# Order of the projected tiles around the HGRN2 heads and the RWKV-7 preparation in a two-layer decoder trunk

## The chip, the cores and the metric

The kernel runs on one core of one Trainium2 chip. The metric is the device time of one execution in microseconds; three executions are shown and their median counts. One execution was taken with the hardware profiler.

## What is computed

Two layers work on a sequence of 512 tokens of width 1024 in float32. Per layer:

```
h    = x * (1 + scale) + shift              (adaLN of the conditioning vector c)
proj = h @ w_in                             (49 column tiles of 128)
q, f, i, z_hg   -> HGRN2, 4 heads of 128    S_t = diag(f_t) S_{t-1} + k_t v_t^T, o_t = S_t^T q_t
                   v = i, k and log f from f, in chunks
r, k, v, z_rw, w, a -> RWKV-7, 8 heads of 64   (token shift on all of them)
y    = (sigmoid(g_A) * y_A + sigmoid(g_B) * y_B) @ w_out
x    = LayerNorm(alpha * x + gate * y)
```

HGRN2's head needs f for its gate f and its key k, q for the query, and i only as the value v. The RWKV-7 preparation needs r, k and v of its two heads.

## The kernel before, in words

Everything is kept transposed, features in partitions and 512 tokens in the free dimension. One projected tile is 128 columns of `w_in` against all of h: `proj` (L252) loads the weights in two halves, splits each into a rounded part (ACT, L120) and a remainder (POOL, L125), and issues 24 matmuls of 512 columns (L261, L262, L266) into one PSUM bank of the pool `pj`, which has two banks. A tile's reader must have emptied a bank before the tile after next may begin.

Each layer runs, for p = 0 to 3, first `hg_head` (L688), one HGRN2 head, and then `rw_prep` (L403), which prepares two RWKV heads. Both are chains of small steps on DVE, ACT and POOL with few matmuls, written as Python generators. `weave` (L277) mixes them with a second generator, the fill, which is the projection of tiles needed later: before part i of the chain it takes `counts[i]` matmuls from the fill, and `issue_after` ties the part's own PE instructions behind the last of them. What is left of the fill runs after the chain. The order on PE is thus written out by hand; the order on the other engines is laid down when the kernel is built, by priority (the order in which the program traces the instructions) among those that are ready and have a buffer. All engine queues are worked off in order.

In `hg_head` the parts are: (1) copies of I and Q, the tanh of F, the gate f and the key K (L697 to L704); (2) four transposes of I (L709) and a copy, then the reciprocal of f's odd columns (L720) and products with f; (3) the first product (L730) and its mask; (4) to (8) five levels that double the block, each with two matmuls (L759), a predicated copy into `acc` (L761), copies of K and Q (L751, L754) and products by `double`; (9) a last level (L775); (10) transposes of K (L785); (11) L792 and the states S; (12) the output products L802 and L805. PSUM pool `hg` has two banks. In `rw_prep` the first part holds the shifts of r, k and v, the second the transposes of L438, the third the products L454 and L455, the fourth L487 and the transposes of v (L494).

Before, the fill of head p is R, K and V of p (72 matmuls; in layer 0 the first R and K come from the start, and I of head 1 joins), and the fill of preparation p is I, Q and F of head p+1 (72), of which `WPR` puts 0 + 4 + 26 + 5 between the parts and 37 come after it. In layer 1 the tiles WA, I and Q are computed at the layer boundary (`next_tiles`, L914) and F runs by itself in front of head 0. The adaLN reductions (L302, with their loads at L321) are filled in on DVE where `ada_next` (L313) places them. Loads of weights are issued on SP's queue (L246).

Of the kernel before, what the change touches and what calls it, by code (L numbers as in the profile page):

```python
# [22 lines left out]
NWARM = 5  # L23
ORD = ((11, 2), (3, 20), (4,), (5, 6), (21,7), (8,), (), ())

WHZ = (0, 2, 0, 7, 0, 15, 5, 0, 7, 1, 7, 12)
WHG = (0, 4, 16, 6, 11, 6, 6, 0, 8, 0, 6, 12)
WPR = (0, 4, 26, 5)
WHN = (0, 19, 0, 11, 11)
WT = (172, 0, 13, 0, 14, 3, 0, 0)  # L30
WCH = (0, 3, 3, 1, 7, 5, 5)
# [50 lines left out]
def body(ctx, tc, d):  # L82
# [20 lines left out]
    def u(shape=(128, 512), dt=F32):  # L103
        return st("u", list(shape), dt)
# [580 lines left out]
        hilo(y, o)  # L685


    def hg_head(l, hd, pf, pq, pi, outs):  # L688


        D_ = dv[l]
        h1, h1n, lbm = (D_[n][:, hd:hd + 1] for n in ("h1", "h1n", "lbm"))
        iv, Qb, Q, th = u(), u(), hl(), u()

        c4 = lambda t, e: t.rearrange("p (c e j) -> p c e j", c=2, e=2)[:, :, e]
        k4 = lambda t, e: c4(t, 1)[:, :, ::-1] if e else c4(t, 0)
        for e in range(2):  # L697
            A.copy(k4(iv, e), c4(pi, e))
        A.copy(Qb, pq)
        act(th, pf, AF.Tanh, scale=0.5)  # L700
        K, f = hl(), u()
        ts(V, f, th, 1.0, h1, ALU.add, ALU.mult)
        ts(V, f, f, lbm, 1e-30, ALU.add, ALU.max)
        ts(G, K, th, h1n, h1, ALU.mult, ALU.add)  # L704

        yield
        pT = ps("hg")
        for t in range(4):
            PE.transpose(pT[:, t * 128:(t + 1) * 128], iv[:, t * 128:(t + 1) * 128], ident)  # L709
        vt = hl()  # L710
        A.copy(vt, pT)
        acc = hl()
        c3 = lambda t: t.rearrange("p (c j) -> p c j", j=128)
        acc3 = c3(acc)
# [31 lines left out]
        for n, H in enumerate(HG_LEVELS):  # L746

            late = lambda t: t.rearrange("p (c b two j) -> p c b two j", c=4, two=2, j=H)[:, :, :, 1]
            lv = u()
            kp, ql = lv[:, 0:256], lv[:, 256:512]  # L750
            A.copy(ql.rearrange("p (c b j) -> p c b j", c=4, j=H), late(Q))  # L751
            for e in range(2):
                k = k4(K, e).rearrange("p c (m f j) -> p c m f j", f=2, j=H)[:, :, :, e]
                PK[e](kp.rearrange("p (c m f j) -> p c m f j", c=2, f=2, j=H)[:, :, :, e], k)  # L754
            w = double(H, w)
            yield
            pS = ps("hg")
            for c in range(2):
                mm(pS[:, c * 128:(c + 1) * 128], kp[:, c * 128:(c + 1) * 128], ql[:, c * 128:(c + 1) * 128],  # L759
                   start=c == 0, stop=c == 1)  # L760
            V.copy_predicated(late(acc), hmask[:, n].rearrange("p (c b j) -> p c b j", c=4, j=H),  # L761
                              pS[:, 0:256].rearrange("p (c b j) -> p c b j", c=4, j=H))
        lv = u()
        kp, ql = lv[:, 0:256], lv[:, 256:512]
        A.copy(ql.rearrange("p (c j) -> p c j", j=64), c3(Q)[:, :, 64:128])
# [13 lines left out]
            A.copy(c4(acc, e)[r, :, 64:128], c4(pS[:, 0:256], e)[r])  # L779
        dec = W[:, w:w + 4]  # L780

        yield
        pT = ps("hg")
        for t in range(3):
            PE.transpose(pT[:, t * 128:(t + 1) * 128], (kr if t == 1 else K[:, t * 128:(t + 1) * 128]), ident)  # L785
# [43 lines left out]

    xs, x1, out = d["x"], d["x1"], d["out"]  # L830
    w_in = d["w_in"]
    first = (CT_WA, CT_I, CT_Q, CT_F, CT_K, CT_R, CT_GH)
    NF = len(first)
    rtag = ("raw", "raw", "raw", "o", "o", "o", "o", "pu", "pu", "pu", "pu", "o", "o", "o")
    utag = (("wh", "wl"), ("wh", "wl"), ("wh", "wl"), ("hl", "hl"), ("hl", "hl"), ("hl", "pr"), ("pr", "pr"),
# [77 lines left out]

    def next_tiles():  # L914

        srcs = [w_in[1, c, h] for c in (CT_WA, CT_I, CT_Q) for h in range(2)]
        tags = (("wh", "wl"), ("wh", "wl"), ("wh", "wl"), ("G", None), ("G", None), ("X", "X"))
        ws, vw = [], []

        def unit():  # L920
            n = len(ws)
            if n == 2 and not vw:
                raw, w = st("raw", [128, 8, 32]), st("bkt", [128, 8, 64], F32R)
                nc.sync.dma_start(raw, d["vdn"])
                act(w[:, :, 0:32], raw, AF.Copy)
                tt(G, w[:, :, 32:64], raw, w[:, :, 0:32].bitcast(F32), ALU.subtract)
                vw.append(w)
                return
            th, tl = tags[n]
            raw = st("raw", [128, 512])  # L930
            nc.sync.dma_start(raw, srcs[n])
            if tl:
                hi, lo = st(th, [128, 512], F32R), st(tl, [128, 512], F32R)
            else:
                g = st(th, [128, 2, 512], F32R)
                hi, lo = g[:, 0], g[:, 1]
            split(raw, hi, lo)
            ws.append((hi, lo))
        def tiles():
            fo.extend([ps("rw"), ps("rw"), ps("pj"), ps("pj")])  # L940
            for th in range(2):
                tk = slice(256 * th, 256 * th + 256)
                for n, o in enumerate(fo):
                    if n == 1:
                        for k in range(8):
                            w = vw[0][:, k]
                            if k < 7:
                                yield mm(o[0:64, tk], w, hT[k][:, 0, tk], start=th == 0 and k == 0, stop=False)
                            yield mm(o[0:32, tk], w[:, 0:32], hT[k][:, 1, tk], start=False, stop=False)
                        yield mm(o[0:64, tk], w, hT[k][:, 0, tk], start=False, stop=th == 1)  # L950
                        continue
                    for k in range(8):
                        hi, lo = (w[:, k % 4 * 128:k % 4 * 128 + 128] for w in ws[2 * (n - (n > 1)) + k // 4])
                        yield mm(o[:, tk], hi, hT[k][:, 0, tk], start=th == 0 and k == 0, stop=False)
                        yield mm(o[:, tk], hi, hT[k][:, 1, tk], start=False, stop=False)
                        yield mm(o[:, tk], lo, hT[k][:, 0, tk], start=False, stop=th == 1 and k == 7)

        fo = []
        return fo, unit, tiles()
# [3 lines left out]
    for l in range(L):  # L963
# [44 lines left out]
                outs.append((yield from ct(c)))  # L1008

        if l == 0:  # L1010
            hgp, rkv = [fout[1], fout[2], fout[3]], [fout[5], fout[4]]
        else:
            hgp, rkv = [fout[2], fout[3]], []
            run(tiles([CT_F], hgp))
        for p in range(NP):
            fill = tiles([c + p for c in (CT_R, CT_K, CT_V)][len(rkv):], rkv)
            pi, pq, pf = hgp
            early = []
            if l == 0 and p == 0:
                fill = itertools.chain(fill, tiles([CT_I + 1], early))  # L1020
            weave(hg_head(l, p, pf, pq, pi, oT), fill, WHZ if l == 0 and p == 0 else WHG)
            run(fill)
            ada_next(*itertools.islice(ada, (WAZ, WAO)[l][2 * p]))
            if p == 0:
                rw["vtm"] = [st("X", [128, 512]) for _ in range(8)]
            hgp = early
            if p < 3:
                fill = tiles([c + p + 1 for c in (CT_I, CT_Q, CT_F)][len(hgp):], hgp)
            else:
                fill = itertools.chain.from_iterable(  # L1030
                    [gate(j) for j in range(5)] + [zrw(p) for p in range(NP)] + [zhg(p) for p in range(NP)] +
                    [gate(j) for j in range(5, KT)])
            weave(rw_prep(l, p, *rkv), fill, WPR)
            ada_next(*itertools.islice(ada, (WAZ, WAO)[l][2 * p + 1]))
            if p < 3:
                run(fill)
            rkv = []
# [293 lines left out]
```

## Time and profile before

| | us |
|---|---|
| three executions | 1029.41, 1031.85, 1032.98 |
| median | 1031.85 |
| the profiled execution, its own time | 1030.67 |
| span of its profile, first to last instruction | 1028.9 |

The span is the profiled execution from its first to its last instruction; 1.8 us of that execution lie around it. A busy share is an engine's share of the span. The granted clock of PE is 1.00 at 2.4 GHz and 0.50 at 1.2 GHz, the only two levels; a value between them is a mean over a stretch. An operation on a timeline is shown with the idle time of its engine just before it and with what ended that idle time. Matmuls overlap in the pipeline: one of 512 columns lasts longer than the distance to the next one.

### The profile page before, as it was taken

To read this page: it belongs to the slowest core of one execution; us is meant where nothing else is said; L and a number is where in the kernel's file an instruction comes from. 1 tells how busy PE (TensorE), PEld (TensorE's weight loads), DVE (VectorE), ACT (ScalarE), POOL (GpSimd) and SP (SyncE) were. 2 spreads that over 40 slices of the span, in tenths; PEclk is the share of its full clock that TensorE was granted. 3 is DMA by queue.
4 is the path that set the end of the run, shared out by engine and by line. 5 is a ranking of instruction groups with operands and counts; after the bars stand their busy time and mean duration, and the time that the engine had idled before them with its cause. 6 is when DMAs were issued, how large, how long until landed. Compare 5 with 4: busy or idle time off the path is not lost.

```text
span 1028.9 us, 16689 instructions
## 1 busy us (share of the span) xinstructions
PE 951.9 (93%) x6132; PEld 761.9 (74%) x6132; DVE 700.1 (68%) x1251; ACT 454.3 (44%) x920; POOL 578.9 (56%) x502
## 2 busy tenths in 40 slices
PE   7988898989989999989999988989999999998997
PEld 4766677878877777757887777777787777776876
DVE  7789986577993444694677867676799544384347
ACT  3456354546325335423356455445642443444321
POOL 5465545345445656768545554545554466576765
PEclk9989899999999999999999999999999999998999
DMA  9824532223321111674535322322232111254422
GB/s 310 301 84 146 170 104 71 80 65 83 92 73 52 53 42 54 194 250 133 184 124 175 113 82 62 83 67 68 62 97 88 53 50 45 92 164 133 123 83 82
DMA packets 61748, 112.83 MB, mean 110 GB/s; under 512 B 6865, under 2 KB 11361, under 8 KB 61666
## 3 DMA queue, kind: packets, MB, share of 16 engines
q1 hardware_dynamic: 57778, 105.12, 33.2%
q10 hardware_dynamic: 3888, 6.64, 2.0%
q8 instruction: 48, 0.79, 0.3%
q14 instruction: 34, 0.28, 0.1%
HBM read 106.49 MB, written 5.25 MB: 109 GB/s over the span
## 4 chain that ended last, share of the span: by engine, by line
PE 44%; DVE 40%; issue 6%; POOL 5%; DMA 3%; ACT 2%; POOLq 0%; DVEq 0%; ACTq 0%; SPq 0%
PE ppj L266 9%; PE ppj L261 9%; PE ppj L262 9%; DVE t L125 4%; DVE z L302 4%; DVE hl L125 3%; DVE t L523 3%; POOL wl L125 3%; DVE u L125 2%; DVE B L302 2%; DVE ar L526 2%; DVE t L515 2%; DVE u L134 1%; PE prw L579 1%; DMA z<-in_w_ada 1%
## 5 line engine op out<-in xcount | busy, mean ns | idle before, releaser
L125 POOL TENSOR_TENSOR wl<-raw,wh 128x512 fp32r<-128x512 f32 (+1 forms) x233 | 318.6, 1372 | 255.7 <-PE ppj L266 107.0
L120 ACT ACTIVATE wh<-raw 128x512 fp32r<-128x512 f32 (+1 forms) x233 | 144.1, 622 | 159.9 <-PE ppj L262 105.1
L261 PE MATMUL ppj<-B,wh 128*128 128x512 f32 x432 | 174.4, 404 | 4.5 <-ACT wh L120 3.9
L262 PE MATMUL ppj<-B,wh 128*128 128x512 f32 x432 | 172.4, 399 | 0.0
L261 PE MATMUL ppj<-A,wh 128*128 128x512 f32 x400 | 164.1, 410 | 5.6 <-ACT t L122 3.7
L262 PE MATMUL ppj<-A,wh 128*128 128x512 f32 x400 | 162.7, 407 | 0.0
L266 PE MATMUL ppj<-B,wl 128*128 128x512 f32 x432 | 126.0, 403 | 2.1 <-POOL wl L125 2.1
L266 PE MATMUL ppj<-A,wl 128*128 128x512 f32 x400 | 117.9, 407 | 1.7 <-POOL wl L125 1.6
L261 PEld LDWEIGHTS ppj<-B,wh 128*128 128x128 f32 x432 | 82.0, 190 | 24.0 <-ACT wh L120 5.9
L262 PEld LDWEIGHTS ppj<-B,wh 128*128 128x128 f32 x432 | 82.1, 190 | 16.2
L261 PEld LDWEIGHTS ppj<-A,wh 128*128 128x128 f32 x400 | 77.4, 193 | 22.5 <-ACT t L122 4.1
L266 PEld LDWEIGHTS ppj<-B,wl 128*128 128x128 f32 x432 | 79.5, 190 | 19.2 <-POOL wl L125 3.8
L262 PEld LDWEIGHTS ppj<-A,wh 128*128 128x128 f32 x400 | 77.5, 194 | 15.4
L266 PEld LDWEIGHTS ppj<-A,wl 128*128 128x128 f32 x400 | 74.5, 192 | 17.6 <-POOL wl L125 3.0
L125 POOL TENSOR_TENSOR hl<-hl,u 128x256 f32<-128x256 f32 x40 | 33.9, 847 | 40.9 <-DVE u L754 24.6
L125 DVE TENSOR_TENSOR t<-t,t 128x144 f32<-128x144 f32 (+29 forms) x62 | 44.8, 723 | 2.1
L759 PE MATMUL phg<-u 128*128 128x128 f32 x160 | 27.7, 300 | 15.6 <-DVE hl L761 13.5
L759 PEld LDWEIGHTS phg<-u 128*128 128x128 f32 x160 | 24.1, 204 | 23.4 <-ACT u L768 14.6
L131 DVE TENSOR_SCALAR u<-u,dvh 128x512 f32<-128x512 f32 x8 | 8.0, 997 | 44.9 <-ACT u L122 44.9
L302 DVE CUSTOM_DVE_ANT_0 z<-z,mbd,prm 128x512 f32<-128x512 f32 x32 | 29.2, 912 | 5.9 <-DMA z<-in_w_ada 3.2
L125 DVE TENSOR_TENSOR hl<-hl,u 128x256 f32<-128x256 f32 x64 | 31.8, 516 | 0.5
L125 DVE TENSOR_TENSOR raw<-raw,X 128x512 f32<-128x512 f32 x8 | 5.9, 742 | 38.5 <-DMA raw<-in_w_out 31.9
(475 smaller groups left out, 1982.4 us busy)
## 6 DMA issues: line engine op xcount, KB each, us to landing
raw<-in_w_in SPq DMA_DIRECT2D x182, 256.0 KB, 2.6
z<-in_w_ada SPq DMA_DIRECT2D x64, 256.0 KB, 3.4
B<-in_w_ada SPq DMA_DIRECT2D x16, 512.0 KB, 6.2
raw<-in_w_br SPq DMA_DIRECT2D x32, 256.0 KB, 2.7
raw<-in_w_out SPq DMA_DIRECT2D x32, 256.0 KB, 3.0
u<-in_x SPq DMA_DIRECT2D x8, 256.0 KB, 3.9
o<-in_w_in SPq DMA_DIRECT2D x14, 128.0 KB, 4.5
t<-in_xt SPq DMA_DIRECT2D x6, 256.0 KB, 3.2
```

Of the source, the lines that this page charges most:

```text
L120: A.activation(out, in_, f, scale=scale)
L125: e.tensor_tensor(o, a, b, op=op)
L134: V.scalar_tensor_tensor(o, a, s, b, op0=op0, op1=op1)
L261: yield mm(o, w, xh, start=half == 0 and k == 0, stop=False)
L262: yield mm(o, w, xl, start=False, stop=False)
L266: yield mm(o, w, xh, start=False, stop=half == n - 1 and k == 3)
L302: V.tensor_tensor_reduce(out=w[h], in0=w[h], in1=silc[h], scale=0.5, scalar=0.0 if h else init, op0=ALU.mult, op1=ALU.add, accum_out=part[ ...
L515: V.transpose(Tin[qs].rearrange("p t s -> p s t"), ax[qs, :, cs_].rearrange("p h s -> p s h"))
L523: V.tensor_reduce(blk(R, t, [32, j]), pv, axis=AX.X, op=ALU.add)
L526: V.transpose(ax[qs, :, cs_].rearrange("p h t -> p t h"), R[qs].rearrange("p j t -> p t j"))
L579: mm(pg[h][:, p * 128:(p + 1) * 128], BK[p][hs, ch], ZR[p][hs, ch], start=p == 0, stop=p == 3)
L759: mm(pS[:, c * 128:(c + 1) * 128], kp[:, c * 128:(c + 1) * 128], ql[:, c * 128:(c + 1) * 128], start=c == 0, stop=c == 1)
```

## The change

The tile order turns round. The fill of preparation p is now F and Q of head p+1 (48 matmuls), and I of a head is projected first in the fill of that head itself, before K, R and V (96 matmuls). In layer 0, preparation 0, all three are still projected there (F in head 0, then Q and I). Layer 1's boundary computes F in place of I, and F no longer runs by itself. In `hg_head` the tanh of F comes first; the copies of I come at its start if I is there, or in the third level; the transposes of I join the third level's group of matmuls; the transposes of K join the last level's. The parts of `hg_head` become 10 in place of 12, and the counts of all weaves over heads and preparations are new.

```diff
--- before.py
+++ after.py
@@ -23,9 +23,11 @@
 NWARM = 5
 ORD = ((11, 2), (3, 20), (4,), (5, 6), (21,7), (8,), (), ())
 
-WHZ = (0, 2, 0, 7, 0, 15, 5, 0, 7, 1, 7, 12)
-WHG = (0, 4, 16, 6, 11, 6, 6, 0, 8, 0, 6, 12)
-WPR = (0, 4, 26, 5)
+WHZ = (0, 4, 4, 4, 6, 6, 7, 7, 5, 5)
+WHG = (0, 14, 5, 7, 8, 8, 9, 9, 7, 8)
+WHL = (0, 26, 4, 6, 7, 7, 9, 9, 7, 8)
+WHS = (0, 10, 4, 5, 6, 6, 7, 8, 6, 6)
+WPR = (0, 4, 20, 6)
 WHN = (0, 19, 0, 11, 11)
 WT = (172, 0, 13, 0, 14, 3, 0, 0)
 WCH = (0, 3, 3, 1, 7, 5, 5)
@@ -685,30 +687,31 @@
         hilo(y, o)
 
 
-    def hg_head(l, hd, pf, pq, pi, outs):
+    def hg_head(l, hd, src, outs):
 
 
         D_ = dv[l]
         h1, h1n, lbm = (D_[n][:, hd:hd + 1] for n in ("h1", "h1n", "lbm"))
-        iv, Qb, Q, th = u(), u(), hl(), u()
+        pf, pq = src[:2]
+        Qb, Q, th = u(), hl(), u()
 
         c4 = lambda t, e: t.rearrange("p (c e j) -> p c e j", c=2, e=2)[:, :, e]
         k4 = lambda t, e: c4(t, 1)[:, :, ::-1] if e else c4(t, 0)
-        for e in range(2):
-            A.copy(k4(iv, e), c4(pi, e))
+        iv = []
+
+        def values():
+            iv.append(u())
+            for e in range(2):
+                A.copy(k4(iv[0], e), c4(src[2], e))
+
+        act(th, pf, AF.Tanh, scale=0.5)
+        if len(src) > 2:
+            values()
         A.copy(Qb, pq)
-        act(th, pf, AF.Tanh, scale=0.5)
         K, f = hl(), u()
         ts(V, f, th, 1.0, h1, ALU.add, ALU.mult)
         ts(V, f, f, lbm, 1e-30, ALU.add, ALU.max)
         ts(G, K, th, h1n, h1, ALU.mult, ALU.add)
-
-        yield
-        pT = ps("hg")
-        for t in range(4):
-            PE.transpose(pT[:, t * 128:(t + 1) * 128], iv[:, t * 128:(t + 1) * 128], ident)
-        vt = hl()
-        A.copy(vt, pT)
         acc = hl()
         c3 = lambda t: t.rearrange("p (c j) -> p c j", j=128)
         acc3 = c3(acc)
@@ -753,6 +756,8 @@
                 k = k4(K, e).rearrange("p c (m f j) -> p c m f j", f=2, j=H)[:, :, :, e]
                 PK[e](kp.rearrange("p (c m f j) -> p c m f j", c=2, f=2, j=H)[:, :, :, e], k)
             w = double(H, w)
+            if n == 2 and not iv:
+                values()
             yield
             pS = ps("hg")
             for c in range(2):
@@ -760,6 +765,13 @@
                    start=c == 0, stop=c == 1)
             V.copy_predicated(late(acc), hmask[:, n].rearrange("p (c b j) -> p c b j", c=4, j=H),
                               pS[:, 0:256].rearrange("p (c b j) -> p c b j", c=4, j=H))
+            if n == 2:
+
+                pT = ps("hg")
+                for t in range(4):
+                    PE.transpose(pT[:, t * 128:(t + 1) * 128], iv[0][:, t * 128:(t + 1) * 128], ident)
+                vt = hl()
+                A.copy(vt, pT)
         lv = u()
         kp, ql = lv[:, 0:256], lv[:, 256:512]
         A.copy(ql.rearrange("p (c j) -> p c j", j=64), c3(Q)[:, :, 64:128])
@@ -779,7 +791,6 @@
             A.copy(c4(acc, e)[r, :, 64:128], c4(pS[:, 0:256], e)[r])
         dec = W[:, w:w + 4]
 
-        yield
         pT = ps("hg")
         for t in range(3):
             PE.transpose(pT[:, t * 128:(t + 1) * 128], (kr if t == 1 else K[:, t * 128:(t + 1) * 128]), ident)
@@ -829,7 +840,7 @@
 
     xs, x1, out = d["x"], d["x1"], d["out"]
     w_in = d["w_in"]
-    first = (CT_WA, CT_I, CT_Q, CT_F, CT_K, CT_R, CT_GH)
+    first = (CT_WA, CT_F, CT_Q, CT_I, CT_K, CT_R, CT_GH)
     NF = len(first)
     rtag = ("raw", "raw", "raw", "o", "o", "o", "o", "pu", "pu", "pu", "pu", "o", "o", "o")
     utag = (("wh", "wl"), ("wh", "wl"), ("wh", "wl"), ("hl", "hl"), ("hl", "hl"), ("hl", "pr"), ("pr", "pr"),
@@ -913,7 +924,7 @@
 
     def next_tiles():
 
-        srcs = [w_in[1, c, h] for c in (CT_WA, CT_I, CT_Q) for h in range(2)]
+        srcs = [w_in[1, c, h] for c in (CT_WA, CT_F, CT_Q) for h in range(2)]
         tags = (("wh", "wl"), ("wh", "wl"), ("wh", "wl"), ("G", None), ("G", None), ("X", "X"))
         ws, vw = [], []
 
@@ -1008,29 +1019,29 @@
                 outs.append((yield from ct(c)))
 
         if l == 0:
-            hgp, rkv = [fout[1], fout[2], fout[3]], [fout[5], fout[4]]
+            hgp, rkv = [fout[1], fout[2], fout[3]], [fout[4], fout[5]]
         else:
             hgp, rkv = [fout[2], fout[3]], []
-            run(tiles([CT_F], hgp))
         for p in range(NP):
-            fill = tiles([c + p for c in (CT_R, CT_K, CT_V)][len(rkv):], rkv)
-            pi, pq, pf = hgp
+            fill = tiles([c + p for c in (CT_K, CT_R, CT_V)][len(rkv):], rkv)
             early = []
+            if len(hgp) < 3:
+                fill = itertools.chain(tiles([CT_I + p], hgp), fill)
             if l == 0 and p == 0:
-                fill = itertools.chain(fill, tiles([CT_I + 1], early))
-            weave(hg_head(l, p, pf, pq, pi, oT), fill, WHZ if l == 0 and p == 0 else WHG)
+                fill = itertools.chain(fill, tiles([CT_F + 1], early))
+            weave(hg_head(l, p, hgp, oT), fill, (WHG if p > 1 else (WHZ, WHS)[p]) if l == 0 else (WHG if p else WHL))
             run(fill)
             ada_next(*itertools.islice(ada, (WAZ, WAO)[l][2 * p]))
             if p == 0:
                 rw["vtm"] = [st("X", [128, 512]) for _ in range(8)]
             hgp = early
             if p < 3:
-                fill = tiles([c + p + 1 for c in (CT_I, CT_Q, CT_F)][len(hgp):], hgp)
+                fill = tiles([c + p + 1 for c in (CT_F, CT_Q, CT_I)[:3 if early else 2]][len(hgp):], hgp)
             else:
                 fill = itertools.chain.from_iterable(
                     [gate(j) for j in range(5)] + [zrw(p) for p in range(NP)] + [zhg(p) for p in range(NP)] +
                     [gate(j) for j in range(5, KT)])
-            weave(rw_prep(l, p, *rkv), fill, WPR)
+            weave(rw_prep(l, p, rkv[1], rkv[0], rkv[2]), fill, WPR)
             ada_next(*itertools.islice(ada, (WAZ, WAO)[l][2 * p + 1]))
             if p < 3:
                 run(fill)
```

## Rows read from the trace of the kernel before

**Rows 1.** The page: engine shares, and the chain that ended last, by engine.

```profile
PE 951.9 (93%) x6132; PEld 761.9 (74%) x6132; DVE 700.1 (68%) x1251; ACT 454.3 (44%) x920; POOL 578.9 (56%) x502
...
PE 44%; DVE 40%; issue 6%; POOL 5%; DMA 3%; ACT 2%; POOLq 0%; DVEq 0%; ACTq 0%; SPq 0%
```

**Rows 2.** Windows, both mixer stages: stretch, length; busy us (count) by engine; clock, DMA, GB/s.

```profile
63.50:246.80 183.30, 164.19 (x912) 134.33 (x912) 144.33 (x291) 96.95 (x218) 91.92 (x84) 0.94 0.35 105
548.00:742.00 194.00, 176.61 (x984) 144.45 (x983) 136.54 (x271) 99.96 (x226) 99.01 (x91) 0.97 0.30 88
```

**Rows 3.** PE's waits over the span: line, whom it waited for, us, times, longest.

```profile
PE phg L759 <- DVE hl L761: 13.5, 11, 2.1
PE phg L730 <- DVE u L125: 10.1, 7, 4.4
...
PE prw L487 <- DVE A L134: 3.8, 3, 2.1
PE phg L805 <- DVE u L134: 3.7, 4, 1.7
...
PE prw L487 <- DVE B L134: 0.4, 1, 0.4
```

**Rows 4.** DVE's waits over the span, the longest.

```profile
DVE u L131 <- ACT u L122: 44.9, 5, 9.3
```

**Rows 5.** PE's timeline, head 2 of layer 0: start, us, operation [idle before, releaser].

```profile
154.65 0.39 PE L261 MATMUL ppj<-A,wh 128*128 128x512 f32 x1
...
157.37 0.39 PE L261 MATMUL ppj<-A,wh 128*128 128x512 f32 x1
...
166.03 1.13 PE L730 MATMUL phg<-u,u 128*128 128x128 f32 x8 [0.78 <-DVE u L125]
...
177.51 0.68 PE L759 MATMUL phg<-u 128*128 128x128 f32 x4 [2.10 <-DVE hl L761]
...
189.86 0.60 PE L438 MATMUL prw<-cc,pu 128*128 128x128 f32 x4
...
197.90 0.69 PE L487 MATMUL prw<-B,B 64*64 64x64 f32 x32
```

**Rows 6.** DVE's timeline of the same head; last, its copies of L754 (min/median/max ns).

```profile
160.92 1.03 DVE L131 TENSOR_SCALAR u<-u,dvh 128x512 f32<-128x512 f32 x1 [8.86 <-ACT u L122]
...
162.92 1.75 DVE L720 RECIPROCAL u<-u 128x256 f32<-128x256 f32 x1
...
171.81 0.74 DVE L134 SCALAR_TENSOR_TENSOR pr<-ppj,prm,pr 128x511 f32<-128x511 f32 x1
...
173.49 0.68 DVE L125 TENSOR_TENSOR B<-pr,ep 128x512 f32<-128x512 f32 x1
...
174.87 1.29 DVE L754 COPY u<-hl 128x128 f32<-128x128 f32 x1
...
L754 DVE COPY u<-hl x10: 209/218/1297, 167.0 to 222.2; 128x128 f32<-128x128 f32 x10
```

**Rows 7.** POOL's timeline, same head.

```profile
174.63 1.45 POOL L125 TENSOR_TENSOR wl<-raw,wh 128x512 fp32r<-128x512 f32 x1
```

**Rows 8.** Windows of three stretches of layer 0, columns as in rows 2.

```profile
96.00:118.80 22.80, 17.95 (x114) 14.29 (x113) 22.48 (x54) 11.06 (x26) 10.63 (x10) 0.96 0.72 233
118.80:142.00 23.20, 22.05 (x110) 18.64 (x111) 21.80 (x54) 11.67 (x29) 11.95 (x11) 0.89 0.34 103
166.00:190.00 24.00, 21.54 (x113) 18.08 (x114) 17.81 (x39) 12.71 (x29) 10.68 (x11) 0.93 0.21 56
```

**Rows 9.** PE's timeline, first product of layer 1's first head.

```profile
563.85 1.75 PE L730 MATMUL phg<-u,u 128*128 128x128 f32 x8 [1.93 <-DVE u L125]
```

**Rows 10.** PE's and DVE's timelines, RWKV preparation 1 of layer 1.

```profile
637.50 0.60 PE L438 MATMUL prw<-cc,pu 128*128 128x128 f32 x4
...
646.60 0.69 PE L487 MATMUL prw<-A,A 64*64 64x64 f32 x32 [0.99 <-DVE A L134]
...
643.65 2.31 DVE L420 TENSOR_TENSOR_SCAN pu<-mask,t 128x512 f32<-128x512 f32 x1
```

## Prediction

> **What bounds the kernel now.** I read the page's engine shares first. PE is busy 93% of the span, and the chain that ended last lies 44% on PE and 40% on DVE [rows 1]: PE is the engine that must not wait, and DVE mostly decides when it does. Nothing in the change adds or removes a projection, so only PE's idle time and its clock can move.
>
> The windows of the two mixer stages, one per layer, come second [rows 2]. PE works 164.19 of 183.30 us in layer 0 and 176.61 of 194.00 us in layer 1, so it is idle for 36.5 us, and the granted clock is 0.94 and 0.97. These stages hold the four heads and four RWKV preparations of each layer, nearly all that the diff touches.
>
> The list of PE's waits names the places [rows 3]: the first product of a head (L730) waited 10.1 us in 7 places for DVE, the products of the levels (L759) 13.5 us in 11, the preparation's L487 3.8 us and 0.4 us, the head's last product (L805) 3.7 us. DVE's own list shows the counterpart [rows 4]: five times it stood idle before L131 for the tanh of F, 44.9 us in all. So F comes late: DVE idles at the end of a preparation because F is the last of three tiles projected, and then PE idles because the chain after F is long.
>
> **One head in time** [rows 5, 6]. Twelve projection products take 157.37 - 154.65 = 2.72 us, 0.227 us each, so a tile of 24 takes 5.4 us. In head 2 of layer 0 the chain starts on DVE at 160.92, after 8.86 us of idleness, and L730 can start at 166.03: 5.1 us, before which the old order puts 20 fill products (4.5 us) and four transposes. It waits 0.78 us. Later L759 of the fourth level waits 2.10 us (177.51).
>
> **The change part by part.** All terms are against the profiled execution, 1030.67 us; the median of the three runs is 1031.85 us, 1.2 us above it.
>
> *F and Q first, I into the head.* What moves with tile I: 24 products, two loads on SP, two weight copies on ACT, two subtractions on POOL (1.45 us in [rows 7]), besides the two ACT copies of I, its four transposes and the ACT copy behind them. The number of each stays. On SP the loads of I move behind those of F and Q and stay in front of those of K, R and V; the adaLN loads keep their place in the program. POOL gets two more subtractions in the head (busy 10.68 of 24.00 us [rows 8]) and two fewer in the preparation. I cost these queues at nothing; what hides them is the products of the tile before, 5.4 us, and without that cover a tile would start up to 1.45 us late.
>
> *A new wait.* The transposes of I now stand in the third level's group, with the products of the fourth level and all later fill queued behind them on PE. They need the two ACT copies of I. I is finished at fill product 24 and they come after 34, 2.3 us later; R's first product, which needs I's PSUM bank, comes 5.4 us later. Cost 0 (0 to +3, should ACT be late by some 0.4 us in each head).
>
> *First product of a head.* After the change F ends 24 products into the preparation's fill, and 6 + 18 + 14 = 38 products (8.6 us) follow before L730, against 20 now. The chain takes 5.1 us and a tanh. Five of the seven waits are 0.8 us or so: 10.1 less the 4.4 us of the longest [rows 3] and the 1.93 us of layer 1's first head [rows 9] leaves 3.8 us. I take -3.8 (0 to -3.8).
>
> *Start of layer 1.* F's 24 products no longer run alone in front of the head; F now comes out of the boundary stage, and 26 products of I and K cover the chain. The 1.93 us wait [rows 9] should go: -2 (0 to -3).
>
> *Layer 0, first to second head.* The 4.4 us wait lies where DVE is full: 22.48 of 22.80 us, then 21.80 of 23.20 us [rows 8]. Behind the wait the clock is 0.89 over 23.20 us, 22% of it at the lower level, 2.6 us lost; the wait and that are 7 us. A full DVE cannot give that back unless the order in its queue improves, for the adaLN reductions stand among the chain. I take -2 (0 to -7).
>
> *Levels.* Fill from L730 to the fourth level's product was 6+11+6+6 = 29 products and becomes 5+7+8+8 = 28 and four transposes, so the cover is the same; the fifth level gets 9 in place of 0. What changes is DVE's load. R is finished at fill product 72 in place of 24 (K at 48 as before), so the shift of R (0.74 us) and its product with the decay (0.68 us) leave this stretch [rows 6]: 1.4 of the 2.10 us. Five heads have such a wait, 10.5 of the 13.5 us: -7. Of the 3.0 us in the six smaller ones I take -1.3, for the fifth level's cover. Three of the five heads show 0.93 as clock over some 24 us, head 2 of layer 0 among them [rows 8]: 14% of it at 1.2 instead of 2.4 GHz, 1.7 us lost each; I take two of the three as returned, -3.4. Sum -11.7 (0 to -17).
>
> On DVE a copy in these levels took 1.29 us at 174.87 where POOL's subtraction ran from 174.63 for 1.45 us, and 0.22 us in the median [rows 6, 7]. The Trainium skill (SBUF — State Buffer, section Who interferes with whom) says that DVE in a two-port mode and GpSimd lock one port pair, and the later one blocks until the other ends. By that rule the term for the levels would come near nothing and the sum near +0.2, since as many subtractions fall into them as before; the second rival has it as a mechanism. The trace agrees on the single copy.
>
> *Last product of a head (L805).* Fill in front of it falls from 12 to 5 (layer 0, head 0), 6 (head 1) or 8. In the steady heads no wait is listed there; the 3.7 us lie in the heads with adaLN reductions. Those lose 7, 6 and 4 products, 3.9 us of cover. I take half: +2 (0 to +4).
>
> *RWKV preparation.* Between its transposes (L438) and L487 the fill falls from 31 to 26 products: 1.1 us less cover. From 189.86 to 197.90 is 8.0 us now, without a wait [rows 5], 6.9 us after. Four of eight preparations wait there already, 4.2 us together [rows 3], and layer 1 shows 9.1 us with 0.99 us of waiting [rows 10]. Those four lose 1.1 us each, and I count in a fifth, the one behind head 1 of layer 0, where DVE is nearly full [rows 8]: +6, rounded up. It may be +2, if DVE gets its reductions done during the 21 products of V that now stand in front, or +15, if V's shift (0.74 us, as [rows 6] has it for R) adds to all eight.
>
> *Sum:* -3.8 - 2 - 2 - 11.7 + 2 + 6 = -11.5 us. 1030.67 - 11.5 = 1019.2, and with the 1.2 us to the median 1020. All good ends: -29; all bad: +22.
>
> **Rivals.**
> 1. *Slower: the chain of F is laid in front of the chain to L487.* F ends at the very place where the preparation's last products on DVE are due, and the order of DVE's queue is fixed when the kernel is built, by what is ready. If the two scalings and the reciprocal, 160.92 to 164.67, 3.75 us [rows 6], stand in front of BK, six preparations (0 to 2 of each layer) wait that much: 6 x 3.75 = 22.5, so 1042. It decides from 2.4 us each, where the 11.5 us and 3.1 us of measurement are used up. For it: the scan of the next preparation, 2.31 us at 643.65, already stands there in layer 1 [rows 10]. Against: F's chain is traced later and so has lower priority.
> 2. *No change: the waits move.* DVE stays full through the levels, its copies held up by POOL's subtractions as at 174.87 [rows 6, 7], and in layer 0's start; likewise if the order laid down leaves the tanh as late as it is, so that the change does not do what it says. Levels and second head give 0: -3.8 - 2 + 2 + 6 = +2.2, so 1034. The port rule named above speaks for this case in the levels.
> 3. *More: DVE's idle 44.9 us are really used.* The shifts run beside V's 21 products, so L487 loses only 2; levels give 14, the second head 5, L805 costs 1: -3.8 - 2 - 5 - 14 + 1 + 2 = -21.8, 1010.
>
> **How the numbers follow.** The forecast has 0.55, rival 1 0.14, rival 2 0.13, rival 3 0.18. A change below 0.3%, 3.1 us, can hardly be told from none. Faster: nearly all of the forecast (0.52), rival 3 (0.18), a little of rival 2: 0.72. Within: 0.12, mostly rival 2. Slower: rival 1 and the rest of 2, 0.16. The range of 1008 to 1034 takes in rivals 2 and 3 and leaves out rival 1 and the good ends.
>
> **What would show it.** Right: the tanh's 44.9 us on DVE nearly gone, L730's waits under 2 us, L759's at 2.1 us fallen below 1, L487's waits grown to about 10 us, the granted clock of layer 0's stage above 0.95, and the two stages, 183.30 and 194.00 us now, some 4 and 7 us shorter. Wrong: L487 above 20 us (rival 1), L759 unchanged at 13 us (rival 2), or a new wait of the projections themselves (L261) for a PSUM bank that I, K or Q still holds.

## The result and the profile after

The changed kernel is slower. Its median is 1047.38 us against 1031.43 us of the kernel before: a ratio of 1.0161, 95% interval 1.0127 to 1.0195. The forecast was 1020, and the range ended at 1034.

Lines of the kernel after are two to eleven higher than before (L261 is now L263, L438 L440, L487 L489, L730 L733, L709 L772, L759 L764, L761 L766, L805 L816, L591 L593). The page's shares, which answer to [rows 1]: span, engines, then the chain that ended last.

```profile
span 1044.1 us, 16675 instructions
PE 953.8 (91%) x6132; PEld 759.5 (73%) x6132; DVE 711.3 (68%) x1251; ACT 455.1 (44%) x920; POOL 576.4 (55%) x502
...
PE 48%; DVE 36%; POOL 6%; issue 5%; ACT 4%; DMA 2%; SPq 0%; POOLq 0%; DVEq 0%; ACTq 0%
```

PE does the same 6132 matmuls in nearly the same busy time (953.8 against 951.9 us) and is idle for longer. PE's waits over the span, in the columns of [rows 3], say where:

```profile
PE ppj L263 <- DVE pr L136: 13.8, 7, 3.3
...
PE prw L593 <- ACT ar L558: 5.6, 2, 3.1
...
PE phg L733 <- DVE u L127: 4.6, 4, 3.5
PE phg L772 <- DVE hl L766: 4.0, 5, 0.8
PE phg L764 <- ACT u L757: 3.7, 1, 3.7
...
PE prw L489 <- DVE A L136: 3.0, 4, 1.0
...
PE phg L764 <- ACT u L754: 2.5, 1, 2.5
...
PE phg L764 <- DVE u L757: 1.7, 5, 0.6
PE prw L489 <- DVE B L136: 1.5, 1, 1.5
```

Three more lines of before belong beside these:

```profile
PE prw L591 <- ACT ar L556: 1.8, 2, 0.9
...
PE phg L759 <- DVE u L754: 1.5, 1, 1.5
...
PE phg L759 <- ACT pr L122: 0.6, 1, 0.6
```

Part of what the forecast wanted has come. A head's first product waits 4.6 us in place of 10.1, L489 waits 4.5 us, about the 4.2 of before, and the five waits of DVE for the tanh of F [rows 4] are no longer listed. In the levels the gain is smaller than it looks: no product of L764 waits for a masked copy any more (13.5 us before), but the transposes of I, which now follow in the third level's group, wait for them 4.0 us (L772), and the other waits of the levels have grown from 2.1 to 7.9 us. Together that is 11.9 us in place of 15.6. The first line of the list is new: a projection waits for a PSUM bank, 13.8 us in seven places. The wait of the first chunk's transposes (L593) for ACT's copies of `ar`, the inverse, is 5.6 us and was 1.8.

The span in four stretches: heads of layer 0, the rest of that layer, heads of layer 1, the rest; kernel before, then after (columns of [rows 2], whose two rows are the first and third stretch of before; the second and fourth are these). The borders lie at the same instructions in both kernels: the transposes of `rw_prep`'s last v, and the start of layer 1's L379 (L381 after).

```profile
246.80:548.00 301.20, 287.75 (x2112) 231.29 (x2112) 198.35 (x308) 124.53 (x230) 179.83 (x144) 1.00 0.37 113
...
742.00:1028.90 286.90, 268.80 (x1946) 214.64 (x1944) 172.63 (x255) 105.58 (x190) 175.52 (x139) 0.98 0.30 92
```

```profile
63.50:246.40 182.90, 162.15 (x907) 131.42 (x907) 144.62 (x291) 95.97 (x218) 92.75 (x86) 0.96 0.35 105
246.40:555.26 308.86, 293.03 (x2117) 235.93 (x2116) 201.03 (x308) 125.43 (x230) 178.75 (x143) 0.98 0.36 110
555.26:752.71 197.45, 175.94 (x979) 141.83 (x978) 141.05 (x271) 100.05 (x226) 99.68 (x90) 0.98 0.31 89
752.71:1044.10 291.39, 270.30 (x1951) 214.33 (x1949) 176.37 (x255) 106.61 (x191) 172.35 (x139) 0.99 0.29 89
```

The differences are -0.4, +7.7, +3.5 and +4.5 us. The counts show that five products have moved from the first stretch to the second and five from the third to the fourth, 1.1 us each time at 0.227 us a product. So the loss is not only in the heads: 12.2 of the 15.2 us lie behind the last preparation of a layer, and 2.3 of these are moved work.

**The new wait.** One place of seven, in head 1 of layer 1: PE, ACT, DVE (timelines, columns of [rows 5]).

```profile
636.83 1.09 PE L268 MATMUL ppj<-B,wl 128*128 128x512 f32 x4
639.49 0.50 PE L263 MATMUL ppj<-B,wh 128*128 128x512 f32 x1 [1.56 <-DVE pr L136]
...
637.96 1.26 ACT L124 ACTIVATE pr<-ppj,dvomm 128x512 f32<-128x512 f32 x2 [0.25 <-PE ppj L268]
...
640.12 0.91 ACT L124 ACTIVATE pu<-pr,prm 128x256 f32<-128x256 f32 x2 [0.90 <-DVE pr L136]
...
638.68 1.41 DVE L136 SCALAR_TENSOR_TENSOR pr<-ppj,prm,pr 128x511 f32<-128x511 f32 x2 [0.80 <-ACT pr L124]
```

At 636.83 PE runs R's last products. The next product, at 639.49, is V's first, and it needs an empty bank. K was finished 24 products earlier, but its bank is still full: both token shifts, r's and k's, stand together on ACT (x2) behind R's end, because the preparation traces `shift(r)` ahead of `shift(k)` while the change projects K ahead of R. So with R's end both banks are full, and V waits until a shift has emptied one. Before, R came first in both orders.

Which bank V then takes, the timeline does not name. V starts when the first of DVE's two steps is done (0.75 us by itself, so at 639.43). K's is the second: the next step of k on ACT (`pu<-pr`) starts at 640.12, at the end of both. So it seems to be R's bank, which is emptied first, and the rule that a tile takes the bank of the tile before last does not hold here. The wait is the same: had k's shift stood ahead, K's bank would have been free long before.

**The late copy.** ACT and PE at the end of layer 0's inversion, and last ACT's same addition in the kernel before:

```profile
314.08 0.63 ACT L124 ACTIVATE u<-z 128x512 f32<-128x512 f32 x1 [3.44 <-POOL z L127]
...
316.05 1.18 ACT L558 COPY ar<-prw 32x512 f32<-32x512 f32 x2 [0.82 <-DVE ar L558]
...
316.68 1.11 PE L593 MATMUL prw<-cc,W 128*128 128x128 f32 x4 [2.56 <-ACT ar L558]
...
312.89 0.63 ACT L122 ACTIVATE u<-z 128x512 f32<-128x512 f32 x1 [0.86 <-POOL z L125]
```

ACT waits 3.44 us (0.86 before) for an addition of POOL on a gate tile (`z`) and only then comes to the copies of `ar`. That gate tile is fill. The generator of gate tiles starts in the last preparation of a layer and runs on through every later stage; with the new `WPR` the preparation takes 30 products from it and not 35, so each later stage meets the gate tiles five products earlier in their course.

### The profile page after: what moved, and what is told of

Same layout as the page of the kernel before. It is cut to its first block, busy times and chain, and to the rows that moved or that the text cites. A ratio compares the mean times of both kernels' runs of the same rounds, so it can differ in the third digit from the quotient of the medians.

```text
span 1044.1 us, 16675 instructions
## 1 busy us (share of the span) xinstructions
PE 953.8 (91%) x6132; PEld 759.5 (73%) x6132; DVE 711.3 (68%) x1251; ACT 455.1 (44%) x920; POOL 576.4 (55%) x502
## 4 chain that ended last, share of the span: by engine, by line
PE 48%; DVE 36%; POOL 6%; issue 5%; ACT 4%; DMA 2%; SPq 0%; POOLq 0%; DVEq 0%; ACTq 0%
PE ppj L263 10%; PE ppj L268 10%; PE ppj L264 9%; DVE t L127 4%; DVE z L304 4%; DVE u L127 3%; POOL wl L127 3%; DVE hl L127 3%; DVE t L525 3%; DVE B L304 2%; DVE t L517 2%; DVE u L136 1%; PE prw L581 1%; DVE ar L528 1%; PE prw L600 1%
## 5 line engine op out<-in xcount | busy, mean ns | idle before, releaser
L263 PE MATMUL ppj<-B,wh 128*128 128x512 f32 x432 | 176.5, 409 | 13.6 <-DVE pr L136 7.4
L263 PE MATMUL ppj<-A,wh 128*128 128x512 f32 x400 | 165.5, 414 | 11.7 <-DVE pr L136 6.4
L268 PE MATMUL ppj<-B,wl 128*128 128x512 f32 x432 | 123.6, 399 | 1.3 <-POOL wl L127 1.3
L263 PEld LDWEIGHTS ppj<-B,wh 128*128 128x128 f32 x432 | 82.3, 191 | 34.1 <-DVE pr L136 9.1
L263 PEld LDWEIGHTS ppj<-A,wh 128*128 128x128 f32 x400 | 77.1, 193 | 30.6 <-DVE pr L136 7.7
L264 PEld LDWEIGHTS ppj<-A,wh 128*128 128x128 f32 x400 | 77.4, 193 | 13.8
L127 DVE TENSOR_TENSOR hl<-hl,u 128x256 f32<-128x256 f32 x64 | 38.2, 613 | 2.1 <-ACT u L754 0.9
L127 DVE TENSOR_TENSOR W<-prw,d 64x256 f32<-64x256 f32 x32 | 13.5, 422 | 37.9 <-PE prw L605 27.0
L136 DVE SCALAR_TENSOR_TENSOR pr<-ppj,prm,pr 128x511 f32<-128x511 f32 x22 | 15.8, 745 | 30.4 <-ACT pr L124 30.4
L764 PEld LDWEIGHTS phg<-u 128*128 128x128 f32 x160 | 24.0, 200 | 15.3 <-ACT u L754 6.7
L764 PE MATMUL phg<-u 128*128 128x128 f32 x160 | 26.9, 293 | 7.9 <-ACT u L757 3.7
L304 DVE CUSTOM_DVE_ANT_0 z<-z,mbd,prm 128x512 f32<-128x512 f32 x32 | 32.1, 1002 | 0.7 <-ACT A L122 0.7
```

The costliest lines, as they stand in the source:

```text
L127: e.tensor_tensor(o, a, b, op=op)
L136: V.scalar_tensor_tensor(o, a, s, b, op0=op0, op1=op1)
L263: yield mm(o, w, xh, start=half == 0 and k == 0, stop=False)
L264: yield mm(o, w, xl, start=False, stop=False)
L268: yield mm(o, w, xh, start=False, stop=half == n - 1 and k == 3)
L304: V.tensor_tensor_reduce(out=w[h], in0=w[h], in1=silc[h], scale=0.5, scalar=0.0 if h else init, op0=ALU.mult, op1=ALU.add, accum_out=part[ ...
```

## The experiments

Theory 1 puts the loss down to the order of the shifts against the order of projection. Theory 2 puts it down to the five products of the last preparation. Theory 3 is for the first heads: adaLN reductions now stand among the levels on DVE, where before they ran while DVE waited for F. Each ratio below is to runs of the kernel before in the same comparison, whose medians were 1031.74, 1032.73 and 1031.81 us.

**k first.**

```diff
-        shift(r, pr, l, p)
         shift(k, pk, l, 4 + p)
+        shift(r, pr, l, p)
```

> The changed kernel with one edit: the RWKV preparation writes k's token shift ahead of r's, in the order in which the changed kernel projects them. Theory 1 (the new wait of V's first product for K's bank, 13.8 us in 7 places, is a matter of that order: both shifts stand on ScalarE behind R's last product, so K's bank stays held until R is through): the wait of the projections on the RWKV buffers drops from 13.8 us to under 3 us, and the time from 1047.4 to 1034 to 1038 us. Rival A (the wait only moves: VectorE is what is late there, and the prepared tiles come no earlier): the V wait goes, the waits for A and B in the preparation and for F of the next head grow by as much, 1045 to 1048 us. Rival B (V's bank is held by the tile before K as much as by K): the wait stays over 8 us, 1044 to 1048 us.

1033.11 us, ratio to before 1.0013 (0.9994 to 1.0033): 14.3 us below the changed kernel and just below the expected range. The projections' wait for the shifts is not listed any more, and the waits of L489 (3.0 and 1.8 us) and L733 (4.3 us) have not taken its place. On ACT k's shift now runs 7 us ahead of r's:

```profile
620.41 0.67 ACT L124 ACTIVATE pr<-ppj,dvomm 128x512 f32<-128x512 f32 x1
...
627.62 0.69 ACT L124 ACTIVATE pr<-ppj,dvomm 128x512 f32<-128x512 f32 x1 [0.25 <-PE ppj L268]
...
627.42 0.39 PE L263 MATMUL ppj<-B,wh 128*128 128x512 f32 x1
```

The last line is V's first product: it waits for nothing and comes ahead of r's shift. Theory 1 holds; both rivals fall.

**Counts of the last preparation.**

```diff
-            weave(rw_prep(l, p, rkv[1], rkv[0], rkv[2]), fill, WPR)
+            weave(rw_prep(l, p, rkv[1], rkv[0], rkv[2]), fill, WPR if p < 3 else (0, 4, 26, 5))
```

> The changed kernel with one edit: the RWKV preparation of the last head of a layer, which has no next head to project for, gets the counts of the kernel before again (0, 4, 26, 5), so that five more gate products stand in it and every later stage of the layer meets the gate tiles at the products at which it met them before. Theory 2 (the 4.3 and 4.4 us lost in the first chunks of the two layers are the gate tile's drains standing ahead of the copies that the inversion waits for, a phase of 5 products): the wait of the inversion for its copy goes from 5.6 us to under 2.5 us, the stretch from the last preparation to the steady chunks shortens by 3 to 4 us in each layer, 1038 to 1041 us. Theory 1 alone: these 8.7 us are from something else, 1045 to 1048 us.

1035.48 us, ratio 1.0033 (1.0017 to 1.005): 11.9 us less than the changed kernel, more than expected. The wait for `ar` is back at its old size, and V's stands unchanged:

```profile
PE ppj L263 <- DVE pr L136: 13.9, 7, 3.3
...
PE prw L593 <- ACT ar L558: 1.8, 2, 0.9
```

Theory 2 holds, but that wait is only 3.8 of the 11.9 us. Windows show where the rest lies. From layer 0's last transposes of v to the first product of its fourth chunk (columns of [rows 2]; before, after, this run):

```profile
245.88:346.52 100.64, 96.92 (x870) 77.20 (x864) 76.44 (x107) 41.34 (x76) 55.06 (x48) 1.00 0.25 72
245.48:349.90 104.42, 99.93 (x868) 79.42 (x864) 77.08 (x107) 42.12 (x77) 50.93 (x45) 0.97 0.24 69
247.31:347.91 100.60, 96.85 (x869) 77.14 (x864) 76.43 (x107) 41.33 (x76) 52.27 (x45) 1.00 0.25 72
```

The change loses 3.8 us here and the old counts give all of it back; the same stretch of layer 1 takes 99.9, 103.7 and 99.9 us, and from layer 0's last chunk to layer 1 it is 155.7, 159.5 and 156.4 us. In layer 0 most of it is the clock: PE is busy 3.0 us longer at 0.97. What let the clock fall there was not tested; with both edits the stretch takes 102.5 us, at 0.97 too.

**The same counts in the kernel before.**

```diff
-            weave(rw_prep(l, p, *rkv), fill, WPR)
+            weave(rw_prep(l, p, *rkv), fill, WPR if p < 3 else (0, 4, 20, 6))
```

> The kernel before with one edit: the last head's RWKV preparation gets the counts of the changed kernel (0, 4, 20, 6), five products fewer. All else of the change is left out. Theory 2: the inversion's wait for its copy appears here too, 1.8 to 5.6 us, and the first chunks take 3 to 4 us more in each layer, 1038 to 1041 us. Theory 1 alone: nothing but the five products' place changes, 1030 to 1033 us.

1041.09 us, ratio 1.0095 (1.0066 to 1.0124), 9.4 us more than the kernel before. The wait appears here too, so these five products cost by themselves:

```profile
PE prw L591 <- ACT ar L556: 5.7, 2, 3.1
```

**K ahead of R in the kernel before**, shifts as they are.

```diff
-            hgp, rkv = [fout[1], fout[2], fout[3]], [fout[5], fout[4]]
+            hgp, rkv = [fout[1], fout[2], fout[3]], [fout[4], fout[5]]
...
-            fill = tiles([c + p for c in (CT_R, CT_K, CT_V)][len(rkv):], rkv)
+            fill = tiles([c + p for c in (CT_K, CT_R, CT_V)][len(rkv):], rkv)
...
-            weave(rw_prep(l, p, *rkv), fill, WPR)
+            weave(rw_prep(l, p, rkv[1], rkv[0], rkv[2]), fill, WPR)
```

> The kernel before with one edit: K is projected ahead of R, while the preparation goes on shifting r ahead of k. The I, Q and F tiles, their order and all counts stay those of before. Theory 1: V's first product now waits for K's bank, some 1.5 to 3.3 us at each of the seven or eight heads, 8 to 14 us in all in the row of the projections' waits, and the time goes to 1039 to 1045 us. Rival B (the order matters only with I also among the fill and its bank in the ring): under 3 us of that wait, 1030 to 1034 us.

1050.75 us, ratio 1.0191 (1.0161 to 1.0221), worse than expected:

```profile
PE ppj L261 <- DVE pr L134: 32.3, 7, 5.0
```

Two swapped tiles cost the kernel before 19.0 us, at least as much as the whole change does. The Trainium skill (Perfetto Trace Analysis, section Matmuls) advises to rotate independent groups of matmuls through PSUM banks, so that emptying one overlaps the next. The row agrees with its purpose and, with the next run, adds a condition for these two banks: the readers must stand in their queue in the order in which the banks fill.

**R ahead of K again in the changed kernel**, with the old counts of the last preparation.

```diff
-            hgp, rkv = [fout[1], fout[2], fout[3]], [fout[4], fout[5]]
+            hgp, rkv = [fout[1], fout[2], fout[3]], [fout[5], fout[4]]
...
-            fill = tiles([c + p for c in (CT_K, CT_R, CT_V)][len(rkv):], rkv)
+            fill = tiles([c + p for c in (CT_R, CT_K, CT_V)][len(rkv):], rkv)
...
-            weave(rw_prep(l, p, rkv[1], rkv[0], rkv[2]), fill, WPR)
+            weave(rw_prep(l, p, *rkv), fill, WPR if p < 3 else (0, 4, 26, 5))
```

> Theory 1 from the other side: the changed kernel with R projected ahead of K, as before the change, and the shifts left as they are (r ahead of k), plus the counts of the last preparation. If only the agreement of the two orders matters, the wait of V's first product is under 3 us and the time is that of both edits, 1019 to 1026 us. If R behind I has a price of its own (its bank was I's, which the transposes free late), a wait of 1 to 3 us per head comes in its place, 1027 to 1034 us.

1021.02 us, ratio 0.9894 (0.9871 to 0.9916): V's wait is not listed. Either order does here, if both agree.

**Both edits**, the two diffs of k first and of the last preparation's counts together.

> The changed kernel with the two edits together: k's token shift written ahead of r's, and the last preparation's counts of the kernel before. Theories 1 and 2 as separate costs: the sum of what each gave alone, 14.3 and 11.9 us, so 1047.4 - 26.2 = 1021 us, between 1018 and 1025, and under the kernel before by about 1.0%. Rival (they overlap: less lateness of the RWKV tiles also takes the sting out of the counts): 1027 to 1032 us. The preparation's counts do not bear on the first heads, so their wait for copies in the levels (3.7 and 2.5 us) should stand unchanged.

1021.12 us, ratio 0.9901 (0.9877 to 0.9925). That is 26.3 us below the changed kernel, where the two alone gave 14.3 + 11.9 = 26.2. Within the noise of these comparisons (2 to 3 us either way) they are separate costs.

**Both edits, adaLN reductions behind the levels.**

```diff
-    pend = []
+    pend, lastlv = [], []
...
-        for g, w in pend:
-            ada_col(*g, w)
+        with ExitStack() as es:
+            if lastlv:
+                es.enter_context(tc.issue_after(lastlv[0].ins))
+            for g, w in pend:
+                ada_col(*g, w)
...
-            V.copy_predicated(late(acc), hmask[:, n] ...
+            lastlv[:] = [V.copy_predicated(late(acc), hmask[:, n] ...
```

> Both edits and a third: the reductions of the next layer's adaLN columns on VectorE, which the changed kernel runs among the levels of the first heads, are ordered behind the last masked copy of the head traced last. Theory 3 (they hold up the first heads' levels): the waits of 3.7 us and 2.5 us for copies in the levels go, 2 to 6 us less than with both edits alone, 1015 to 1019 us. Rival (the levels are late in the first heads for ScalarE's copies of another stage, or the reductions come due behind the head where the preparation needs VectorE): the two waits stay or the preparation's waits for A and B grow by as much, 1020 to 1025 us.

1017.31 us, ratio 0.986 (0.983 to 0.989). The two waits of the first heads' levels (3.7 and 2.3 us with both edits alone) are gone, though 1.7 and 1.5 us of other waits stand there, and the last product of a head pays: 8.2 us (L819 here), where both edits alone have 2.1.

```profile
PE phg L819 <- DVE u L136: 8.2, 10, 2.8
```

The intervals of the two kernels overlap, so the 3.8 us between them are not clear of noise.

**The changed kernel with the reductions behind the levels alone**, by the diff above without the two others.

> The changed kernel with the adaLN reductions behind a head's levels, and nothing else. Theory 3 by itself: the two waits of 3.7 and 2.5 us in the first heads' levels go here too, 1047.4 - 4 = 1043 us, 1040 to 1045. If V's wait takes it back (in the first heads VectorE's lateness and the bank's are one queue): 1045 to 1050 us, with V's wait above 13.8 us.

1049.47 us, ratio 1.0171 (1.0131 to 1.0211): no gain, and V's wait is 20.5 us in place of 13.8. Theory 3 names a wait that exists, but moving the reductions only moves it; it falls as a cost of its own.

**Both edits, I back among the preparation's products** behind F and Q.

```diff
-                fill = tiles([c + p + 1 for c in (CT_F, CT_Q, CT_I)[:3 if early else 2]][len(hgp):], hgp)
+                fill = tiles([c + p + 1 for c in (CT_F, CT_Q, CT_I)][len(hgp):], hgp)
...
-            weave(rw_prep(l, p, rkv[1], rkv[0], rkv[2]), fill, WPR if p < 3 else (0, 4, 26, 5))
+            weave(rw_prep(l, p, rkv[1], rkv[0], rkv[2]), fill, (0, 4, 26, 5))
```

> Both edits, and the next head's I goes back into the fill of the preparation (behind F and Q, so F stays first), with 35 products woven there in every preparation as in the kernel before; each head then has 72 products and not 96 for its levels. What is left of the change is the order of F, Q and I and the group that the transposes of I joined. If most of the gain is F being early (tanh and the reads of the base): the wait of a head's first product stays under 5 us, 1020 to 1026 us, much like both edits. If it is the 24 more products under the levels: the wait for the levels' masked copies and reads grows by 8 to 12 us again, 1029 to 1034 us.

1017.58 us, ratio 0.9862 (0.9839 to 0.9886), below the expected range: the levels do not need the 24 more products. No product of L764 waits for a masked copy, and the transposes at L772 wait for them 1.9 us. A first product waits once, 3.4 us, in the second head of layer 0.

**This with the reductions behind the levels too**, the last two diffs together.

> All four edits: k's shift first, the last preparation's old counts, I back among the preparation's products, and the adaLN reductions behind a head's levels. If what the last two gave (3.8 and 3.5 us beyond both edits) are separate costs: 1021.1 - 3.8 - 3.5 = 1014 us, 1011 to 1016. If the reductions only mattered because the levels had more products over them, or if late reductions meet the preparation: 1016 to 1020 us.

1016.15 us, ratio 0.9847 (0.9806 to 0.9888): not to be told from the one above.

**The order of F, Q and I alone**, in the kernel before, for heads 1 to 3.

```diff
-        for e in range(2):
-            A.copy(k4(iv, e), c4(pi, e))
-        A.copy(Qb, pq)
-        act(th, pf, AF.Tanh, scale=0.5)
+        if hd:
+            act(th, pf, AF.Tanh, scale=0.5)
+            A.copy(Qb, pq)
+        for e in range(2):
+            A.copy(k4(iv, e), c4(pi, e))
+        if not hd:
+            A.copy(Qb, pq)
+            act(th, pf, AF.Tanh, scale=0.5)
...
-            pi, pq, pf = hgp
+            pi, pq, pf = hgp if p == 0 else hgp[::-1]
...
-                fill = itertools.chain(fill, tiles([CT_I + 1], early))
+                fill = itertools.chain(fill, tiles([CT_F + 1], early))
...
-                fill = tiles([c + p + 1 for c in (CT_I, CT_Q, CT_F)][len(hgp):], hgp)
+                fill = tiles([c + p + 1 for c in (CT_F, CT_Q, CT_I)][len(hgp):], hgp)
```

> The kernel before with the order of the next head's tiles alone: F, Q, I in place of I, Q, F for heads 1 to 3 of a layer (F of the second head of layer 0 projected early in place of its I), tanh and Q's copy ahead of I's copies. Old counts, old group of transposes, R ahead of K, old first heads. If the early F is where the gain is: the wait of a head's first product (10.1 us in 7 places) falls under 4 us, and tanh's 44.9 us on VectorE goes by at least half; the waits of the levels (13.5 us) stay as they are, since they belong to the levels' counts and the transposes' group: 1022 to 1027 us. If the early F gives nothing without the other parts (the head is as late, only at its levels): 1029 to 1034 us.

1015.40 us, ratio 0.9849 (0.9805 to 0.9894): 16.4 us below the kernel before (1031.81 in that comparison), with its counts, groups and R ahead of K untouched. It is as fast as the best of the mended versions and beats both kernels. Its waits (here L734, L763 and L809 are L730, L759 and L805 of before) and its two stretches of heads, which hold the same 912 and 984 matmuls as [rows 2]:

```profile
PE phg L734 <- DVE u L125: 5.9, 4, 2.8
PE phg L763 <- ACT u L769: 4.6, 6, 1.4
...
PE phg L763 <- DVE hl L765: 3.4, 7, 1.0
PE prw L487 <- DVE A L134: 3.3, 3, 1.6
...
PE phg L809 <- DVE u L134: 2.5, 4, 1.2
```

```profile
63.50:239.20 175.70, 158.72 (x912) 130.31 (x912) 146.84 (x290) 95.87 (x218) 91.00 (x84) 0.98 0.36 109
...
543.10:725.50 182.40, 172.05 (x984) 142.33 (x983) 140.30 (x271) 98.42 (x226) 97.94 (x91) 0.99 0.32 94
```

The heads are 7.6 and 11.6 us shorter than [rows 2]. The expectation that the levels' waits would stay at 13.5 us was wrong: the wait for the masked copy falls to 3.4 without new counts. In head 2 of layer 0 the DVE chain now starts 13.2 us ahead of the first product (165.81), where before it was 5.1:

```profile
152.65 0.48 DVE L131 TENSOR_SCALAR u<-u,dvh 128x512 f32<-128x512 f32 x1
```

That head start is the likely reason, though no run separates it. Other waits of L763 and L809 come to 9.5 us (4.6, 1.8, 0.6 and 2.5), where before they were 5.8.

## Why the prediction was wrong

Two steps failed. "A new wait" put the cost of the PSUM banks at nothing, and the runs showed 14.3 us. "RWKV preparation" costed the new counts inside that stage alone, and the runs showed 11.9 us, nearly all of it behind the stage. With the two missed costs taken out the change gives 1021.12 us against the forecast of 1020, and the order of the tiles alone 1015.40. That the first comes so near is partly luck, since the other terms were off in both directions.

- **The missing term: V's bank.** "A new wait" asked who holds I's bank when R needs it, and stopped short of V. "Levels" noted that the shift of R would "leave this stretch" and booked that as a gain, without asking where K's shift stands in ACT's queue behind it. The price is 14.3 us (k first), in the shape that the last sentence of the prediction named as proof of error.
- **Counts that were costed for their cover alone.** "RWKV preparation" took the fall from 31 to 26 products as 1.1 us of lost cover at L487, for +6 us. L489 waits 4.5 us in place of 4.2: nothing. But in the last preparation of a layer those products come from a generator that also feeds the inversion, the chunks and the output stages, and taking five fewer there cost 11.9 us (9.4 us when done alone in the kernel before, 1041.09 - 1031.74). The prediction had no term behind the mixer stages at all.
- **First product of a head, start of layer 1, second head:** the wait fell by 5.5 us of the 3.8 + 2 + 2 that were taken. Layer 1's start has none left; the second head of layer 0 keeps 3.5 of its 4.4 us.
- **Levels:** taken as 8.3 us less wait and 3.4 us of clock. All waits there fell by 3.7 us (15.6 to 11.9): those for masked copies from 13.5 to 4.0, while others grew from 2.1 to 7.9, 6.2 of these in the first heads of the two layers. The reason named, R's shift leaving the stretch, was not needed: the early F alone takes 10.1 of the 13.5 us, with R ahead of K. The fill of I under them was not needed either (1017.58 us without it).
- **Last product of a head:** taken as 2 us more wait; L816 waits 0.6 us in place of 3.7, probably because PE comes late itself. Where V's wait is mended it is 2.1 us (both edits).
- **Rivals.** Rival 1 put the slower side at L487, behind the chain of F; those waits did not grow. Rival 2 left the levels as they were; their waits for masked copies fell, though other waits took back more than half of it. The rule of the Trainium skill beside it (SBUF — State Buffer, section Who interferes with whom) was read too simply, since as many subtractions in the heads need not meet as many copies. Before, seven of DVE's 40 copies took 1.27 to 1.30 us, each beside a subtraction of POOL, and five of these started 2.6 us ahead of the five waits of 2.1 us; after, and with the order alone, the longest takes 0.64 us. So up to 1.1 us of each of those five waits may have gone with the meeting. With I back in the preparation five copies take 1.31 us again, and the transposes at L772 wait only 0.4 us each. DVE's copies, before and after:

```profile
L754 DVE COPY u<-hl x40: 209/217/1299, 73.8 to 718.9; 128x128 f32<-128x128 f32 x40
...
L757 DVE COPY u<-hl x40: 212/218/641, 73.6 to 722.3; 128x128 f32<-128x128 f32 x40
```

What stays open: the change less the two costs (1021.12) is 5.7 us above the order alone (1015.40). Which of I's place, the transposes' group and the counts of the heads makes it was not separated. In the two profiled executions the granted clock differs as well, 0.977 and 0.984.

## What to carry to other kernels

When tiles change places, write down for every PSUM bank who empties it and where that reader stands in its engine's queue; the order of projection and the order in which the readers are traced must be changed together. A count that takes work from a shared fill generator moves everything that draws on it afterwards, so it is costed at the far end too. And try the smallest part of a change by itself first: here the order of three tiles gave as much as any version that was run.

## What the runs showed that was not expected

A wait of PE can go with a loss of nearly its own length again, by the clock. Head 2 of layer 0 in the kernel before, in windows of 2 us (columns of [rows 2]):

```profile
174.00:176.00 2.00, 1.41 (x7) 0.80 (x5) 2.00 (x3) 1.10 (x3) 2.00 (x2) 1.00 0.00 0
176.00:178.00 2.00, 0.49 (x4) 0.52 (x4) 1.90 (x7) 1.02 (x5) 0.08 (x1) 1.00 0.44 92
178.00:180.00 2.00, 1.68 (x8) 1.42 (x7) 1.15 (x4) 1.19 (x3) 1.31 (x2) 0.62 0.10 39
180.00:182.00 2.00, 2.00 (x7) 1.57 (x5) 2.00 (x5) 0.72 (x1) 0.73 (x1) 0.53 0.47 118
```

PE is busy 1.41 and then 0.49 of 2 us at full clock, with the wait of 2.10 us at its end [rows 5]; in the next 4 us the clock is 0.62 and 0.53, nearly all at 1.2 GHz, which loses 0.76 + 0.94 = 1.7 us more. Seven stretches at the lower level, of 3.4 or 6.8 us each, lie in the heads of before. Not every wait is followed by one: the changed kernel's seven waits for a bank last 1.6 to 3.3 us, and the clock of its two stages of heads is 0.96 and 0.98, where it was 0.94 and 0.97. With the order of the tiles alone PE's busy time in the two stages of heads, for the same matmuls, is 158.72 and 172.05 in place of 164.19 and 176.61 us: 10.0 of the 19.2 us gained there. The prediction took 3.4 us for it in the levels.

With F early, what DVE waits for in the heads is POOL, no longer the tanh. Order alone, DVE's waits over the span:

```profile
DVE u L758 <- POOL hl L125: 25.8, 13, 4.7
```

Before, the same line was:

```profile
DVE u L754 <- POOL hl L125: 5.1, 8, 0.9
```
